# Hybrid decoder layer, prompt and samples together: a fourth buffer for cached keys and values, sample values in four steps, a rearranged tail

## The chip, the cores and the metric

The kernel runs on one core of a Trainium2 chip. A core has five engines with an instruction queue each: TensorE (PE; its weight loads are listed as PEld), VectorE (DVE), ScalarE (ACT), GpSimd (POOL) and SyncE (SP), which issues most of the transfers. The metric is the time of one execution on the device in microseconds, lower is better. Before the change three runs took 1103.71, 1103.06 and 1101.36 us: median 1103.06.

## The reference

One layer works on a prompt of 512 tokens and on 8 samples of 8 tokens each (64 tokens), with width 1024 and shared weights, all in fp32.

```python
def hybrid_layer(x, mem_k, mem_v, ...):
    u = _rms(x) * g_pre_mix
    proj = u @ w_in
    ...
    mix = jnp.concatenate([y_ssd, h_ml], axis=-1) @ w_out
    x = x + _rms(mix) * g_post_mix
    u = _rms(x) * g_pre_x
    qx = (u @ w_xq).reshape(bsz, length, X_HEADS, X_HEAD_DIM)
    sc = jnp.einsum('blhd,bmhd->bhlm', qx, mem_k) * (X_HEAD_DIM ** -0.5)
    pr = jax.nn.softmax(sc, axis=-1)
    o = jnp.einsum('bhlm,bmhd->blhd', pr, mem_v).reshape(bsz, length, X_WIDTH) @ w_xo
    x = x + _rms(o) * g_post_x
    u = _rms(x) * g_pre_ffn
    f = (jax.nn.silu(u @ w_gate) * (u @ w_up)) @ w_down
    x = x + _rms(f) * g_post_ffn
```

The change lies in the cross-attention and in the last line. The memory has 256 positions, 4 heads of 256. The prompt's memory keys and values are computed (`u @ w_mem_k`, `u @ w_mem_v`, both also outputs); each of the 8 samples brings its own keys and values from a cache, 1 MB of keys and 1 MB of values for each sample. `_rms` divides by the root of the mean square plus 1e-6.

## The kernel before, in words

Activations are held transposed, features on the 128 partitions and the 576 tokens as columns: the prompt in columns 0 to 511, the samples in the last 64. Column halves are worked on one after the other. Each large product is made of three matmuls: an fp32 weight is split into a high part `whi`, cast by ScalarE (line 181), and a rest `wlo`, which VectorE and GpSimd subtract (line 188); the activation likewise. TensorE then forms high·high (L202), high·low (L203) and low·high (L205) for each of the 8 blocks of 128 features, so 24 matmuls make one 128-row output block. Raw weights come in 512 KB loads into a ring of two buffers (`raw`, L176); `whi` and `wlo` have rings of three. A scheduler at build time sets the order of instructions on each engine in most of the program. In the stretches under `tc.manual_schedule` it follows a list of due times written in the kernel.

The cross-attention runs over the heads h = 3, 2, 1, 0. For each head come two query blocks `xq(2h+1)` and `xq(2h)` (24 matmuls each for this column half), the memory keys `mem_key` (48 matmuls, tiles `ps_mk`), the values of the previous head `attn_values` (transposes `ps_pt` and products `ps_ov`), the scores `attn_scores` (`ps_at`) and the memory values `mem_value` (L783 and its neighbours, `ps_v`).

The samples' attention is woven into this. `hb` is a half of the samples, four samples each. `pick` takes for each sample two 512 KB loads of its cached keys or values (`cached`, L1314, issued on SP's queue), and does eight matmuls for it with a 32-column weight (L1327, two trace rows for each matmul), one per head and feature half, that write to four row groups of one PSUM bank. It yields four times in all, after each sample, so a step is two loads, eight matmuls and, after every second sample, the masked adding up by VectorE (L1335, L1337). Two PSUM banks, `B0` and `B1`, take turns. The loads cycle through three places of 4 KB per partition in the tile of slot 5, named `kva` in the trace: each `dma_start` must wait until the matmuls that read its place are done.

`attn_samples_k` is the scores of the samples (`ps_sa`), then softmax and two transposes (`ps_pts`). `attn_samples_v` is the product with the values (`ps_os`), then two transposes (`ps_ots`, L1363) and the copies into `oh` and `ol`, the activations of the output projection. In the loop over h, four `next(steps)` take the steps of `attn_samples_k`: half 1 within h = 2 and half 0 within h = 1. `attn_samples_v` is called whole at the end of h = 1 (half 1) and of h = 0 (half 0); where its instructions then stand on TensorE is for the scheduler to decide.

The output projection `xo` follows: j = 0 to 7, each 24 matmuls of 288 columns (`ps_xo`) in the first column part, weights `wxo`. ScalarE takes squares and the scaled result out of PSUM (L268, L1443). `u3l`, an activation of the FFN stage, takes slot 5 after the sample attention is done with it.

At the end, the down projection's last column part (256 prompt tokens) runs by a list of due times. For each block j, `evac0` adds the partial sums (L2080), squares them (L2083) and scales them by the norm's gain (L2084). `root` sums the squares over the features (L2054), and forms v = sum/1024 + eps (L2057, VectorE) and y = sqrt(v) (L2058, ScalarE); `root_end` makes r ≈ 1/sqrt(v) of it by a reciprocal and one Newton step (L2062 to L2065). `f_rows` transposes the result to tokens on partitions (`ps_ft`, L2114), `last` scales by r and adds the residual (L2130), and the output is stored. One quarter of the output goes through ScalarE (`scaled`) and VectorE (`scaled_add`, L2143) instead.

Of the kernel before, what the change touches and what calls it, by code (L numbers as in the profile page):

```python
# [11 lines left out]
F32 = mybir.dt.float32  # L12
F32R = mybir.dt.float32r
BF16 = mybir.dt.bfloat16
AF = mybir.ActivationFunctionType
ALU = mybir.AluOpType
# [3 lines left out]
P = 128  # L20
# [5 lines left out]
EPS = 1e-6  # L26
# [90 lines left out]
def build(nc, tc, ctx, I, O):  # L117
    V, A, G, S, TE = nc.vector, nc.scalar, nc.gpsimd, nc.sync, nc.tensor
# [12 lines left out]
    def SL(slot, name, dt=F32, shape=(P, KT, T)):  # L131

        return big.tile(list(shape), dt, name=name, tag="s%d" % slot, bufs=1)
# [30 lines left out]
    def PAR(k, j=None, w=1):  # L164
        a, b = _cols[k]
        return par[:, a:b] if j is None else par[:, a + j:a + j + w]

    ident, identb, sel, ones = C32("ident"), C16("identb"), C16("sel"), C32("ones")
# [136 lines left out]
    for k in range(KT):  # L305
        if k % 2 == 0:
            c = slice(128 * k, 128 * k + 256)
# [6 lines left out]
        if k % 2 == 0:  # L314
# [4 lines left out]
                                     op0=ALU.mult, op1=ALU.subtract)  # L319
# [244 lines left out]
    y = xs  # L564
# [100 lines left out]
    for g in range(2):  # L665
        ps = BP("ps_xts")
# [5 lines left out]
    ps = BP("ps_bts")  # L672
# [7 lines left out]
    for g in range(2):  # L680
        for hb in range(2):
            dst = cpad[:, g, 4 * hb:4 * hb + 4, :].rearrange("p b t -> p (b t)")
            src = bc[:, 2 + g, TP + 32 * hb:TP + 32 * hb + 32]
# [4 lines left out]
    for g in range(2):  # L688
# [13 lines left out]
        for h in range(8):  # L702
            k, j = h % 2, (8 * g + h) // 2
# [6 lines left out]
    ps = BP("ps_eg")  # L710
# [7 lines left out]
    for b in range(4):  # L718
# [9 lines left out]
        for hb in range(2):  # L728
# [4 lines left out]
            for g in range(2):  # L733
                ps = BP("ps_hu")
# [6 lines left out]
    ps = BP("ps_yt")  # L741
# [89 lines left out]
    for h in range(4):  # L831
# [17 lines left out]
        for c in range(4):  # L849
# [3 lines left out]
                        op=ALU.mult)  # L853
        num = mp_.tile([P, 4, 257], F32, name="num", tag="num", bufs=2)
        for c in range(4):
# [10 lines left out]
            else:  # L866
                V.scalar_tensor_tensor(cn[:, 0:257], cprev[:, 0:257], scalem[:, c, h:h + 1], psc[:, 0:257],
                                       op0=ALU.mult, op1=ALU.add)
# [42 lines left out]
    for hb in range(2):  # L911
        r = slice(32 * hb, 32 * hb + 32)
# [5 lines left out]
        for b in range(4):  # L918
# [9 lines left out]
            for h in range(4):  # L928
                ps = BP("ps_cu")
                mm(ps[:, 0:258], km[:, h * P:(h + 1) * P], vst[:, h * 258:(h + 1) * 258], start=True, stop=True)  # L930
                V.scalar_tensor_tensor(cn[:, h, :], c0[:, h, :], es[:, h, 8 * bb + 7:8 * bb + 8], ps[:, 0:258],
                                       op0=ALU.mult, op1=ALU.add)
# [94 lines left out]
    for j in range(8):  # L1027
        hm = qk[:, 4 * (j % 2) + j // 2, 0:TP]
        with tc.issue_after((evs[0] if j > 2 else htc).ins):
            A.activation(mixm_h[:, j, 0:TP], hm, AF.Copy, scale=ghalf[:, j:j + 1])  # L1030
        V.scalar_tensor_tensor(mixm_l[:, j, 0:TP], hm, ghalf[:, j:j + 1], mixm_h[:, j, 0:TP].bitcast(F32),
                               op0=ALU.mult, op1=ALU.subtract)
# [160 lines left out]
    m = out2(7, 0)  # L1193
    with tc.issue_after(m.ins):
        rc = rstd_cols([ssq], HCHUNKS[1], "po1", alloc=B0)
    m = out2(6, 0)
# [9 lines left out]
    s5 = SL(5, "kva", F32, (P, 4608))  # L1206
# [98 lines left out]
            split(oh[:, j, 0:TP], ol[:, j, 0:TP], pso)  # L1305


    kv = [s5[:, 1024 * i:1024 * i + 1024] for i in range(3)]
    turn = [0]

    def cached(src):
# [5 lines left out]
    def pick(dst, hb, src, lhs, name):  # L1317

        for pair in range(2):
            ps = (B0, B1)[pair](name)  # L1320
            for b2 in range(2):
                b = 2 * pair + b2
                o = ps[:, 256 * b2:256 * b2 + 256]
                for d in range(2):
                    t_ = cached(src[4 * hb + b, :, d])
                    for h in range(4):
                        mm(o[32 * h:32 * h + 32, :], lhs(h, d), t_[:, h, :], start=d == 0, stop=d == 1,  # L1327
                           skip_group_check=True)
                if not b2:
                    yield  # L1330
            for b2 in range(2):
                b = 2 * pair + b2
                o = ps[:, 256 * b2:256 * b2 + 256]
                if b == 0:
                    V.tensor_scalar(dst, o, C32("bmask")[:, 0:1], None, op0=ALU.mult)  # L1335
                else:
                    V.scalar_tensor_tensor(dst, o, C32("bmask")[:, b:b + 1], dst, op0=ALU.mult, op1=ALU.add)  # L1337
            if not pair:
                yield

    def attn_samples_k(hb):
        pr, pt = s5[:, 3072 + 256 * hb:3328 + 256 * hb], s5[:, 3584 + 256 * hb:3840 + 256 * hb]
        yield from pick(pr, hb, I["kc"], lambda h, d: qsm[:, 2 * h + d, 32 * hb:32 * hb + 32], "ps_sa")
        mx = at.tile([P, 1], F32, name="mxs")
        sm = at.tile([P, 1], F32, name="sms")
        V.reduce_max(mx, pr, axis=AX.X)
        V.tensor_scalar(mx, mx, -1.0 / 16.0, None, op0=ALU.mult)
        A.activation(pr, pr, AF.Exp, scale=1.0 / 16.0, bias=mx, accum_out=sm)
        V.reciprocal(sm, sm)
        V.tensor_scalar(pr, pr, sm, None, op0=ALU.mult)  # L1350
        pst = (B0, B1)[hb]("ps_pts")
        for m in range(2):
            TE.transpose(pst[:, m * P:(m + 1) * P], pr[:, m * P:(m + 1) * P], ident)
        A.copy(pt, pst[:, 0:256])

    def attn_samples_v(hb):
        pt, ot = s5[:, 3584 + 256 * hb:3840 + 256 * hb], s5[:, 4096 + 256 * hb:4352 + 256 * hb]
        tt = slice(TP + 32 * hb, TP + 32 * hb + 32)
        for _ in pick(ot, hb, I["vc"], lambda h, m: pt[:, m * P + 32 * h:m * P + 32 * h + 32], "ps_os"):
            pass  # L1360
        pst = (B0, B1)[hb]("ps_ots")
        for dv in range(2):
            TE.transpose(pst[:, dv * P:(dv + 1) * P], ot[:, dv * P:(dv + 1) * P], ident)  # L1363
        p4 = pst[:, 0:256].rearrange("p (d h t) -> p h d t", d=2, h=4)
        oh4 = oh[:, :, tt].rearrange("p (h d) t -> p h d t", d=2)
        ol4 = ol[:, :, tt].rearrange("p (h d) t -> p h d t", d=2)
        A.copy(oh4, p4)
        V.tensor_tensor(ol4, p4, oh4.bitcast(F32), op=ALU.subtract)

    mk, m = mem_key(3, wm[:2])  # L1370
    with tc.issue_after(m.ins):
        rc = rstd_cols([ssq], HCHUNKS[0], "po0", alloc=B0)
    mv, m = mem_value(3, wm[2:])
# [10 lines left out]
    m = xq(4, 1)  # L1384
    with tc.issue_after(m.ins):
        rc2[1] = rstd_cols([ssq2], HCHUNKS[1], "p21", alloc=B1)
    m = xq(5, 1)
    with tc.issue_after(m.ins):
        rstd_rows(rc2[1], HCHUNKS[1], rb2, B1)
    m = xq(6, 1)  # L1390
    with tc.issue_after(m.ins):
        rc2[0] = rstd_cols([ssq2], HCHUNKS[0], "p20", alloc=B1)
    m = xq(7, 1)
# [6 lines left out]
    steps = iter(())  # L1400
    for h in range(3, -1, -1):

        xq(2 * h + 1, 0)
        next(steps, None)
        xq(2 * h, 0)
        next(steps, None)
        if last:
            mk = mem_key(h)
            next(steps, None)
            attn_values(*last)  # L1410
            next(steps, None)
        pr = attn_scores(h, mk)
        if last:
            mv = mem_value(h)
        last = h, pr, mv
        if h > 1:
            steps = attn_samples_k(h - 2)
        else:
            attn_samples_v(h)
    attn_values(*last)  # L1420
    st.close()

# [23 lines left out]

    u3_ = SL(3, "u3h", F32R, (P, 5120))
    u3h = u3_[:, 0:KT * T].rearrange("p (k t) -> p k t", t=T)
    u3l = SL(5, "u3l", F32R)
    rb, rb3 = rb_tile("px_rb"), rb_tile("p3_rb")  # L1450
    ssq3 = ssq_tile("ssq3")
    x_d = dr.tile([P, KT, T], F32, name="x_d")
# [4 lines left out]
    for j in range(8):  # L1457
        step = xo(j, 0, wx if 3 < j < 7 else None)
        if j < 3:

            step(0, KT - 2)
            with tc.issue_after(ends[-1].ins) if j else ExitStack():
                ends.append(step(KT - 2, KT)[0])
        else:
            ends.append(step(0, KT)[0])


    plan = []

    def at_(p, fn, *a):  # L1470
        plan.append((p, len(plan), lambda: fn(*a)))
# [177 lines left out]
    for n_, (key, p) in enumerate(order):  # L1649
        src = I[{"xo": "wxo", "g": "wgate", "u": "wup"}[key[0]]][key[1]]  # L1650
# [315 lines left out]
    with tc.manual_schedule(engines={TE.engine, A.engine, V.engine, G.engine, S.engine}):  # L1966
# [4 lines left out]
        fp = ctx.enter_context(tc.tile_pool(name="ffn", bufs=1, reuse_waits="tile"))  # L1971
        gt = fp.tile([P, 8, 288], F32, name="gt")
        sw = fp.tile([P, 1024], F32, name="sw")
# [8 lines left out]
    f2 = SL(4, "f_ffn")  # L1982
# [62 lines left out]

    plan = []
    tail, squares = {}, {}

    def root(name, terms, chunks):

        n, ps = len(chunks), B0("ps_ss")
        for m, (t_, b) in enumerate(terms):
            for c, (t0, _) in enumerate(chunks):
                mm(ps[:, c:c + 1], t_[:, t0 - b:t0 - b + P], ones, start=m == 0 and c == 0, stop=m == len(terms) - 1, skip_group_check=True)  # L2054
        v, y, a, r = [fp.tile([P, n], F32, name=name + k) for k in ("_v", "_y", "_a", "_r")]
        tail[name] = v, y, a, r
        V.tensor_scalar(v, ps[:, :n], 1.0 / 1024.0, EPS, op0=ALU.mult, op1=ALU.add)  # L2057
        A.activation(y, v, AF.Sqrt)  # L2058

    def root_end(name):  # L2060
        v, y, a, r = tail[name]
        V.reciprocal(y, y)  # L2062
        V.tensor_tensor(a, y, y, op=ALU.mult)
        V.scalar_tensor_tensor(a, a, -0.5, v, op0=ALU.mult, op1=ALU.mult)
        V.scalar_tensor_tensor(r, a, 1.5, y, op0=ALU.add, op1=ALU.mult)  # L2065
        tail[name] = r

    def root_rows1():
# [9 lines left out]
    def evac0(j):  # L2078
        fj = f2[:, j, 0:256]
        V.tensor_tensor(fj, fj, tail[j], op=ALU.add)  # L2080
        if j:
            squares[j] = ph.tile([P, 320], F32, name="sq", tag="sq", bufs=2)[:, :256]
        A.activation(squares[j] if j else ssqf[:, 0:256], fj, AF.Square)  # L2083
        A.activation(fj, fj, AF.Copy, scale=PAR("g_postffn", j))  # L2084

    def sum0(j):
        V.tensor_tensor(ssqf[:, 0:256], ssqf[:, 0:256], squares[j], op=ALU.add)
# [20 lines left out]
    parts = [(c, d) for c in range(2) for d in range(2)]  # L2108
    xr, xt, ft = [], {}, {}

    def token_rows(src, i, ps):
        c, d = parts[i]
        for j in range(4):
            TE.transpose(ps[:, j * P:(j + 1) * P], src[:, 4 * d + j, c * P:(c + 1) * P], ident)  # L2114
        return ps.rearrange("p (j k) -> p j k", j=4)

    def x_rows(i):
# [4 lines left out]
    def x_copy(i):  # L2122
        A.copy(*xt[i])

    def f_rows(i):
        ft[i] = token_rows(f2, i, (MP if i % 2 else GP)("ps_ft"))

    def last(i):
        o, rc = xt[i][0], tail["pf0"][:, parts[i][0]:parts[i][0] + 1]
# [16 lines left out]
    for i in range(4):  # L2146
        at_(4.0 + i, x_rows, i)
        at_(4.55 + i, x_copy, i)
        at_((7.35, 8.7)[i % 2] + i / 100, f_rows, i)
    at_(8.4, lambda: root("pf0", [(ssqf, 0), (squares[7], 0)], HCHUNKS[0]))  # L2150
    at_(8.8, root_end, "pf0")
    at_(9.0, scaled)
# [115 lines left out]
```

## Time and profile before

| | |
|---|---|
| runs, median (lowest to highest) | 1103.06 us (1101.36 to 1103.71) |
| the profiled execution's own time | 1101.67 us |
| its span in the trace | 1099.9 us |
| granted TensorE clock | 0.998 of full |
| TensorE busy | 1088.4 us (99%), 8355 matmuls |
| VectorE busy | 755.0 us (69%) |
| ScalarE busy | 610.4 us (55%) |
| GpSimd busy | 229.9 us (21%) |
| loads of cached keys (values) | 16 (16) of 512 KB, median 6.4 (7.1) us from issue to landing |

How to read it: the profiled execution is one execution with the hardware's profiler on. Its span, from the first instruction to the last, is 1.8 us less than its own time. Matmuls are pipelined: the row of one matmul shows the time from its start until its result is through, which is longer than the distance to the start of the next. So TensorE's real pace is read from start to start, and a "busy" share of 99% still contains short waits. In a row of the timeline the brackets give the idle time before it and what ended it. The chain that ended last is a walk back from the last instruction, at each step to whatever released it; its shares add up to the span.

### The profile page before, as it was taken

To read this page: it belongs to the slowest core of one execution; us is meant where nothing else is said; L and a number is where in the kernel's file an instruction comes from. 1 tells how busy PE (TensorE), PEld (TensorE's weight loads), DVE (VectorE), ACT (ScalarE), POOL (GpSimd) and SP (SyncE) were. 2 spreads that over 40 slices of the span, in tenths; PEclk is the share of its full clock that TensorE was granted. 3 is DMA by queue.
4 is the path that set the end of the run, shared out by engine and by line. 5 is a ranking of instruction groups with operands and counts; after the bars stand their busy time and mean duration, and the time that the engine had idled before them with its cause. 6 is when DMAs were issued, how large, how long until landed. Compare 5 with 4: busy or idle time off the path is not lost.

```text
span 1099.9 us, 21201 instructions
## 1 busy us (share of the span) xinstructions
PE 1088.4 (99%) x8355; PEld 1041.6 (95%) x8355; DVE 755.0 (69%) x1506; ACT 610.4 (55%) x1106; POOL 229.9 (21%) x305
## 2 busy tenths in 40 slices
PE   9999999999999999999999999999999999999997
PEld 9999888998999999999988889999999999999997
DVE  6896776558877764669655456676567877787555
ACT  6877523346654564656444445645467467656654
POOL 1443544223212112000233301100011111111000
PEclk9999999999999999999999999999999999999999
DMA  6775544334745348653468755644475777678532
GB/s 208 189 150 126 154 144 154 125 96 146 208 140 158 82 152 276 206 201 97 160 234 287 264 188 182 223 154 104 115 175 138 157 187 171 140 174 194 122 129 87
DMA packets 58536, 181.29 MB, mean 165 GB/s; under 512 B 6428, under 2 KB 11676, under 8 KB 57924
## 3 DMA queue, kind: packets, MB, share of 16 engines
q1 hardware_dynamic: 42308, 136.88, 37.5%
q0 software_dynamic: 15552, 41.95, 19.6%
q8 instruction: 65, 1.06, 0.4%
q10 hardware_dynamic: 576, 1.11, 0.3%
q14 instruction: 35, 0.29, 0.1%
HBM read 159.26 MB, written 20.65 MB: 164 GB/s over the span
## 4 chain that ended last, share of the span: by engine, by line
PE 95%; DMA 3%; DVE 1%; ACT 0%; issue 0%; DVEq 0%; ACTq 0%
PE ps_in L202 7%; PE ps_in L203 7%; PE ps_in L205 6%; PE ps_o L202 3%; PE ps_o L205 3%; PE ps_o L203 3%; PE ps_u L1777 3%; PE ps_u L1779 3%; PE ps_u L1778 3%; PE ps_g L1777 3%; PE ps_g L1779 3%; PE ps_g L1778 3%; PE ps_v L784 2%; PE ps_v L783 2%; PE ps_v L782 2%; PE ps_dn L1777 2%
## 5 line engine op out<-in xcount | busy, mean ns | idle before, releaser
L202 PE MATMUL ps_in<-uh,whi 128*128 128x320 f32 (+1 forms) x544 | 163.6, 301 | 0.0
L205 PE MATMUL ps_in<-uh,wlo 128*128 128x320 f32 (+1 forms) x544 | 163.5, 301 | 0.0
L203 PE MATMUL ps_in<-ul,whi 128*128 128x320 f32 (+1 forms) x544 | 162.6, 299 | 0.0
L181 ACT CAST whi<-raw 128x1024 fp32r<-128x1024 f32 (+1 forms) x102 | 102.8, 1011 | 91.6 <-PE ps_in L203 28.5
L188 DVE TENSOR_TENSOR wlo<-raw,whi 128x512 fp32r<-128x512 f32 (+1 forms) x94 | 94.6, 1007 | 62.9 <-ACT whi L181 54.5
L202 PEld LDWEIGHTS ps_in<-uh,whi 128*128 128x128 f32 x544 | 103.2, 190 | 2.3 <-issue 1.7
L205 PEld LDWEIGHTS ps_in<-uh,wlo 128*128 128x128 f32 x544 | 103.0, 190 | 1.1 <-issue 0.4
L203 PEld LDWEIGHTS ps_in<-ul,whi 128*128 128x128 f32 x544 | 103.1, 190 | 0.6
L186 POOL DMA_DIRECT2D wlo<-win x32 | 27.8, 877 | 86.8 <-ACT wlo L185 78.7
L1777 PE MATMUL ps_u<-b,whi 128*128 128x288 f32 x144 | 42.5, 296 | 0.0
L1778 PE MATMUL ps_g<-b,whi 128*128 128x288 f32 x144 | 42.4, 295 | 0.0
L1778 PE MATMUL ps_u<-b,whi 128*128 128x288 f32 x144 | 42.4, 295 | 0.0
L1777 PE MATMUL ps_g<-b,whi 128*128 128x288 f32 x144 | 42.2, 296 | 0.0
L202 PE MATMUL ps_xo<-qh,whi 128*128 128x288 f32 x128 | 38.6, 303 | 0.0
L1750 ACT CAST whi<-rawx 128x1024 fp32r<-128x1024 f32 (+1 forms) x26 | 25.6, 986 | 23.4 <-PE ps_dn L1778 13.0
L202 PE MATMUL ps_o<-mixs_h,whi 128*128 128x320 f32 (+1 forms) x128 | 38.2, 298 | 0.0
L205 PE MATMUL ps_o<-mixm_h,wlo 128*128 128x256 f32 (+1 forms) x128 | 38.1, 298 | 0.0
L203 PE MATMUL ps_xq<-u2l,whi 128*128 128x320 f32 (+1 forms) x128 | 38.1, 299 | 0.0
L203 PE MATMUL ps_o<-mixm_l,whi 128*128 128x256 f32 (+1 forms) x128 | 38.0, 297 | 0.0
L202 PE MATMUL ps_o<-mixm_h,whi 128*128 128x256 f32 (+1 forms) x128 | 37.9, 296 | 0.0
L205 PE MATMUL ps_xq<-u2h,wlo 128*128 128x320 f32 (+1 forms) x128 | 37.9, 296 | 0.0
L202 PE MATMUL ps_xq<-u2h,whi 128*128 128x320 f32 (+1 forms) x128 | 37.8, 299 | 0.0
(762 smaller groups left out, 3919.1 us busy)
## 6 DMA issues: line engine op xcount, KB each, us to landing
raw<-win SPq DMA_DIRECT2D x35, 512.0 KB, 3.7
raw<-wout SPq DMA_DIRECT2D x17, 512.0 KB, 3.9
kva<-kc SPq DMA_DIRECT2D x16, 512.0 KB, 6.4
kva<-vc SPq DMA_DIRECT2D x16, 512.0 KB, 7.1
raw<-wxq SPq DMA_DIRECT2D x13, 512.0 KB, 3.5
raw<-wgate SPq DMA_DIRECT2D x13, 512.0 KB, 5.8
raw<-wup SPq DMA_DIRECT2D x13, 512.0 KB, 4.9
wlo<-win POOLq DMA_DIRECT2D x24, 256.0 KB, 5.5
```

What stands on the lines that cost most here:

```text
L181: A.copy(hi[:, :n], raw[:, :n])
L186: G.dma_start(lo[:, a:b], src[:, a:b], accum_op=ALU.add)
L188: e.tensor_tensor(lo[:, a:b], raw[:, a:b], hi[:, a:b].bitcast(F32), op=ALU.subtract)
L202: mm(ps, wh, ah, start=i == 0, stop=False)
L203: mm(ps, wh, al, start=False, stop=False)
L205: m = mm(ps, tiles[order[c]][1], xh(order[c], t0, n), start=False, stop=c == len(tiles) - 1)
L782: mm(o, ah, hi[:, j:j + 256], start=k == 0, stop=False, skip_group_check=True)
L783: mm(o, al, hi[:, j:j + 256], start=False, stop=False, skip_group_check=True)
L1750: A.copy(s.h3[:, s.all], s.r2[:, s.all])
L1777: mm(ps, wh, b[0][k], start=start and k == 0, stop=False, skip_group_check=True)
L1778: mm(ps, wh, b[1][k], start=False, stop=False, skip_group_check=True)
L1779: m = mm(ps, wl, b[0][k], start=False, stop=k == nk - 1, skip_group_check=True)
```

## The change

Three things are changed.

1. The cached keys and values get a fourth place, a tile `kvb` from a pool of its own that is closed after the first column part of the output projection. `u3l` is allocated after that.
2. `attn_samples_v` yields as `attn_samples_k` does. Half 1's steps are taken within h = 0 and half 0's within the output projection, one after each `xo(j, 0)`, j = 0 to 7 (as long as there are any).
3. In the tail, `root` lets ScalarE take the square root from PSUM directly (scale 1/1024, eps as a bias tile), and VectorE forms v and its reciprocal; `root_end` has three operations instead of four. For block j = 7 the scaled copy is VectorE's, into another buffer, instead of ScalarE's in place. Of the transposes for odd i, the first three blocks are due before the root's sums (8.2), the last one after them (8.7).

```diff
-    kv = [s5[:, 1024 * i:1024 * i + 1024] for i in range(3)]
+    kxs = ExitStack()
+    kx = kxs.enter_context(tc.tile_pool(name="kx", bufs=1, side="right", reuse_waits="tile"))
+    kv = [s5[:, 1024 * i:1024 * i + 1024] for i in range(3)] + [kx.tile([P, 1024], F32, name="kvb")]
...
     def attn_samples_v(hb):
...
-        for _ in pick(ot, hb, I["vc"], lambda h, m: pt[:, m * P + 32 * h:m * P + 32 * h + 32], "ps_os"):
-            pass
+        yield from pick(ot, hb, I["vc"], lambda h, m: pt[:, m * P + 32 * h:m * P + 32 * h + 32], "ps_os")
...
         last = h, pr, mv
-        if h > 1:
-            steps = attn_samples_k(h - 2)
-        else:
-            attn_samples_v(h)
+        steps = attn_samples_k(h - 2) if h > 1 else attn_samples_v(h)
     attn_values(*last)
...
-    u3l = SL(5, "u3l", F32R)
...
             ends.append(step(0, KT)[0])
+
+        next(steps, None)
+    kxs.close()
+    u3l = SL(5, "u3l", F32R)
...
+    eps = fp.tile([P, 1], F32, name="eps")
+    V.memset(eps, EPS)
...
         tail[name] = v, y, a, r
+        A.activation(y, ps[:, :n], AF.Sqrt, scale=1.0 / 1024.0, bias=eps)
         V.tensor_scalar(v, ps[:, :n], 1.0 / 1024.0, EPS, op0=ALU.mult, op1=ALU.add)
-        A.activation(y, v, AF.Sqrt)
+        V.reciprocal(v, v)
 
     def root_end(name):
+
         v, y, a, r = tail[name]
-        V.reciprocal(y, y)
-        V.tensor_tensor(a, y, y, op=ALU.mult)
-        V.scalar_tensor_tensor(a, a, -0.5, v, op0=ALU.mult, op1=ALU.mult)
-        V.scalar_tensor_tensor(r, a, 1.5, y, op0=ALU.add, op1=ALU.mult)
+        V.tensor_tensor(a, y, v, op=ALU.mult)
+        V.scalar_tensor_tensor(r, a, -0.5, y, op0=ALU.mult, op1=ALU.mult)
+        V.scalar_tensor_tensor(r, r, 1.5, a, op0=ALU.add, op1=ALU.mult)
         tail[name] = r
...
         A.activation(squares[j] if j else ssqf[:, 0:256], fj, AF.Square)
-        A.activation(fj, fj, AF.Copy, scale=PAR("g_postffn", j))
+        if j < 7:
+            A.activation(fj, fj, AF.Copy, scale=PAR("g_postffn", j))
+        else:
+            V.tensor_scalar(sw[:, 512:768], fj, PAR("g_postffn", j), None, op0=ALU.mult)
...
-    def token_rows(src, i, ps):
+    def token_rows(src, i, ps, js=range(4)):
         c, d = parts[i]
-        for j in range(4):
-            TE.transpose(ps[:, j * P:(j + 1) * P], src[:, 4 * d + j, c * P:(c + 1) * P], ident)
+        for j in js:
+            t_ = sw[:, 512 + c * P:640 + c * P] if src is f2 and 4 * d + j == 7 else src[:, 4 * d + j, c * P:(c + 1) * P]
+            TE.transpose(ps[:, j * P:(j + 1) * P], t_, ident)
...
-        at_((7.35, 8.7)[i % 2] + i / 100, f_rows, i)
+        if i % 2:
+
+            at_(8.2 + i / 100, f_rows, i, range(3))
+            at_(8.7 + i / 100, f_rows, i, range(3, 4))
+        else:
+            at_(7.35 + i / 100, f_rows, i)
```

More of the change, by code (lines that the diff above doesn't have):

```diff
@@ L2123, in x_copy, with f_rows @@
         A.copy(*xt[i])
-    def f_rows(i):
-        ft[i] = token_rows(f2, i, (MP if i % 2 else GP)("ps_ft"))
+    def f_rows(i, js=range(4)):
+        if 0 in js:
+            tail["ft", i] = (MP if i % 2 else GP)("ps_ft")
+        ft[i] = token_rows(f2, i, tail["ft", i], js)
     def last(i):
```

## The prediction

> **What bounds the kernel now.** I read the page first, its chain of work, then the chain of waits and TensorE's timeline around the lines that change.
>
> ```profile
> span 1099.9 us, 21201 instructions
> ...
> PE 95%; DMA 3%; DVE 1%; ACT 0%; issue 0%; DVEq 0%; ACTq 0%
> ```
>
> TensorE sets the end; transfers own 3% of the chain. No matmul is removed, so only time in which TensorE stands still, and the tail behind its last matmul, can be won. The chain between 540 and 670 us shows where it stands still in the changed region (start, length, what):
>
> ```profile
> 579.55 6.03 DMA kva<-kc
> ...
> 594.36 5.98 DMA kva<-kc
> ...
> 612.10 6.05 DMA kva<-vc
> ...
> 637.50 5.84 DMA kva<-vc
> ...
> 655.52 1.23 DVE wlo L188
> 656.76 3.58 DMA raw<-wxo
> 660.36 1.06 ACT whi L181
> 661.50 1.24 DVE wlo L188
> ```
>
> Each piece of 6 us runs from the issue of a load to its landing; TensorE worked through most of it. What it lost is read from the matmul before each place and the one that waited (start, length, engine, line, operation):
>
> ```profile
> 584.90 0.28 PE L205 MATMUL ps_mk<-memhl,wlo 128*128 128x256 f32 x1
> 585.63 0.64 PE L1327 MATMUL ps_sa<-kva,qsm 128*32 128x256 f32 x8 [0.45 <-DMA kva<-kc]
> ...
> 600.00 0.28 PE L1276 MATMUL ps_at<-mk,qh 128*128 128x256 f32 x1
> 600.38 0.64 PE L1327 MATMUL ps_sa<-kva,qsm 128*32 128x256 f32 x8
> ...
> 616.76 0.28 PE L202 MATMUL ps_mk<-memhl,whi 128*128 128x256 f32 x1
> 618.19 0.64 PE L1327 MATMUL ps_os<-kva 128*32 128x256 f32 x8 [1.14 <-DMA kva<-vc]
> ...
> 643.02 0.29 PE L205 MATMUL ps_xo<-qh,wlo 128*128 128x288 f32 x1
> 643.38 0.64 PE L1327 MATMUL ps_os<-kva 128*32 128x256 f32 x8
> ...
> 662.12 0.29 PE L203 MATMUL ps_xo<-ql,whi 128*128 128x288 f32 x1
> 662.77 0.40 PE L205 MATMUL ps_xo<-qh,wlo 128*128 128x288 f32 x1 [0.36 <-DVE wlo L188]
> ```
>
> The normal distances, and what a burst of sample matmuls costs, come from undisturbed places:
>
> ```profile
> 578.52 0.28 PE L203 MATMUL ps_xq<-u2l,whi 128*128 128x256 f32 x1
> 578.64 0.28 PE L205 MATMUL ps_xq<-u2h,wlo 128*128 128x256 f32 x1
> 578.86 1.07 PE L1327 MATMUL ps_sa<-kva,qsm 128*32 128x256 f32 x16
> 579.86 0.39 PE L202 MATMUL ps_xq<-u2h,whi 128*128 128x256 f32 x1
> ...
> 546.31 1.05 PE L1327 MATMUL ps_sa<-kva,qsm 128*32 128x256 f32 x10
> 547.29 0.39 PE L1274 MATMUL ps_at<-mk,qh 128*128 128x256 f32 x1
> ```
>
> A 256-column matmul starts 0.12 us after the one before; the entry into a burst takes 0.22. Start to start less about 0.21 (0.23 and 0.13 among 288-column matmuls), the five places lose 0.52, 0.17, 1.22, 0.13 and 0.52: 2.56 us, 2.04 of it on cached keys and values, the last on a weight of the output projection. That is all there is to win here: 0.23% of the time.
>
> **The change part by part.** *Fourth place and values in steps.* All sixteen loads of keys and sixteen of values stay, with their 128 matmuls. A step takes two loads; with four places a step's pair is issued as the step two before it lets go of its places, so it has one whole step and the work between. For the fourth step of a head that work is 48 matmuls of the memory keys (5.8 us), a 16-row step (1.0) and the transposes of the text's weights (about 1 us), with entries about 8.1 us from the end of step two, and the first place is let go half a step earlier. What stands against it is SP's one queue:
>
> ```profile
> 580.54 4.48 SPq L176 DMA_DIRECT2D raw<-wmv  x2
> 585.11 0.38 SPq L1314 DMA_DIRECT2D kva<-kc  x1
> ...
> 582.87 1.79 POOL L188 TENSOR_TENSOR wlo<-raw,whi 128x512 fp32r<-128x512 f32 x1 [4.06 <-ACT whi L181]
> ...
> DMA to landing us min/median/max: 3.8/6.7/8.0
> ```
>
> For h=1 the second wmv load stands in the queue ahead of the pair of step four and must wait until POOL has read the raw buffer (582.87 + 1.79 = 584.66). So the pair goes out at 585.1 and 585.5 as the single load did before. Step two begins near 583.0 (24 matmuls after 579.9), step four at about 592.0, its second load is wanted at 592.5. By the median of 6.7 us the loads land at 591.8 and 592.2 and nothing waits; by the maximum of 8.0, at 593.5, the wait is 1.0. Bounds 0 and 1.0; the last of several stacked loads is nearer the maximum than the first, so I take **0.4**, in place of 0.52 + 0.17. Queued behind a waiting matmul is all of TensorE. h=2 has no second weight ahead of its pair (none). For h=0:
>
> ```profile
> 614.53 0.72 SPq L1314 DMA_DIRECT2D kva<-vc  x1
> ```
>
> the pair is issued there around 614.1 and 614.5, and with 6.7 us lands at 620.8 and 621.2; step four needs it from 621.8 on. The 1.22 goes. At the maximum of 8.0 it would keep 0.3 to 0.7. The values of h=0 are spread over the projection and loaded from about 639.5, wanted from 649.6: the 0.13 goes. The projection's weight chain (655.52 to 662.74 in the chain above) starts when the block j=0 is done; a burst that stood ahead of that end now stands behind it, about 1.3 us of cover against 0.52 of wait: that goes too. If not, 0.52 stays. So 2.56 is removed and 0.4 returns.
>
> *Bursts.* Two rows are one matmul here. Sixteen rows take 1.00 us (578.86 to 579.86; the row's 1.07 has 0.07 of pipeline behind it), so eight take 0.64 − 0.07 = 0.57 (row 585.63) and eight more add 0.43. What a burst costs beside its rows is then 0.57 − 0.43 = 0.14 within, 0.10 at the entry (0.22 for 0.12) and about 0.1 at the exit (the matmul behind it 0.39 long for 0.28): about 0.33. The changed program has 22 bursts for 24: −0.66. But in the projection they are cut to 6, 2, 2, 4, 3 and 7 matmuls, and the ten rows at 546.31 took 0.98, as much as sixteen: a group of four matmuls that is not full costs as a full one (0.43). The six odd bursts hold 24 matmuls, six groups, and take up eight: +0.86. I take the sum of the two, **+0.2**, with −0.66 and +0.86 as ends. The first load of the fourth place is issued some 150 us early, beside the loads of the output weights; no matmul there waits for a load that it delays by more than its slack. Price 0; uncovered, one load's 0.38 us issue.
>
> *The tail.* VectorE's, ScalarE's and TensorE's rows of before:
>
> ```profile
> 1092.25 0.16 DVE L2057 TENSOR_SCALAR pf_v<-ps_ss 128x2 f32<-128x2 f32 x1 [1.15 <-PE ps_ss L2054]
> 1092.68 0.17 DVE L2062 RECIPROCAL pf_y<-pf_y 128x2 f32<-128x2 f32 x1 [0.27 <-ACT pf_y L2058]
> ...
> 1093.28 0.16 DVE L2065 SCALAR_TENSOR_TENSOR pf_r<-pf_a,pf_y 128x2 f32<-128x2 f32 x1
> 1093.47 0.75 DVE L2130 SCALAR_TENSOR_TENSOR raw<-ps_ft,pf_r,raw 128x512 f32<-128x512 f32 x1
> ...
> 1091.14 0.42 ACT L2083 ACTIVATE sq<-f_ffn 128x256 f32<-128x256 f32 x1 [2.00 <-DVE f_ffn L2080]
> 1091.59 0.51 ACT L2084 ACTIVATE f_ffn<-f_ffn,par 128x256 f32<-128x256 f32 x1
> 1092.44 0.20 ACT L2058 ACTIVATE pf_y<-pf_v 128x2 f32<-128x2 f32 x1 [0.35 <-DVE pf_v L2057]
> ...
> 1092.08 1.07 PE L2114 MATMUL ps_ft<-c,f_ffn 128*128 128x128 f32 x8
> ```
>
> From the root's sum to the last scaling lie 1.22 us: v (0.19 with its gap), root (0.24), reciprocal and three products (0.20 each). The edit means the root on ScalarE and v with its reciprocal on VectorE to run side by side; then the chain is the longer arm (0.39) and three products, 0.99: −0.24. But in the changed program's order VectorE's v waits for ScalarE's root, because both read the same bank of PSUM. Root, v, reciprocal and three products stand in a row again: 1.23, and up to 0.09 more if the bias given as a tile costs what the scale given as a tile costs (0.51 against 0.42). I take **+0.05**, ends −0.24 and +0.10. The Trainium skill, "PSUM — Partial Sum Buffer", section "PSUM bank collisions raise a hardware error", says why that wait has to be there: ScalarE and VectorE may not touch one bank at a time and nothing arbitrates. By that rule the sum is +0.05, without it −0.24; no run here shows the collision.
>
> The moved copy for j=7 fits VectorE's idle 1.15 us before v (0.42 wanted). The earlier transposes fill TensorE's pause before the sums; they were done at 1093.15 anyway, before the factor at 1093.45, so that gains nothing. Without the cover the copy would cost its 0.42.
>
> **Sum.** −2.56 + 0.4 + 0.2 + 0.05 = −1.9 us. The profiled execution took 1101.67 (span 1099.9, 1.8 around it), which becomes 1099.8. It lies 1.4 under the median of the runs, 1103.06, and on that the sum gives **1101.1**.
>
> **The rivals.** *All gains come:* no wait is left, bursts gain 0.66 and the tail's two readers run in parallel: −2.56 − 0.66 − 0.24 = −3.5, 1099.6. For it: 0.4 and 0.2 are small corrections that I chose between ends. Against: the order of the tail.
>
> *The waits only move:* loads now go in pairs, so the second of a pair lands later than a single load would. With 8.0 us for the last one, 1.0 is lost in h=1 and in h=0 each, 0.52 stays at the weight: −2.56 + 2.5 + 0.25 = +0.2, 1103.3. That is the case in which the change does not do what it says. For it: the maximum in the row; against: 6.0 us in the chain.
>
> *Slower:* one mechanism, SP's queue. The two wmv loads, the pair of step three and that of step four are six transfers in a row.
>
> ```profile
> 637.00:644.00 7.00, 6.93 (x70) 5.57 (x62) 2.83 (x5) 3.23 (x8) 1.04 (x1) 1.00 0.82 249
> ```
>
> The last column is GB/s: at 249 a load of 0.524 MB takes 2.11 us. The first out at 580.0 lands after 3.58 (the wxo row); five more at 2.11 end at 594.1, against 592.5 wanted: 1.6 lost, in h=2, h=1 and h=0 each. With the 0.52 that stays: −2.56 + 4.8 + 0.5 + 0.25 = +3.0, 1106.1. It loses 2.2 us or more from 2.06 us for a load on. Against it: single loads stacked up landed after 6 us, not 8.
>
> **How the numbers follow.** A measurement of this kernel tells no change from one of 0.2%, 2.2 us. Forecast 0.50, its own range 1100.2 to 1102.1 by the ends of its terms (faster 0.22, within 0.28). All gains 0.25 (0.24 and 0.01). Waits move 0.11 (within 0.10, slower 0.01). Queue 0.14 (within 0.02, slower 0.12). Together faster 0.46, within 0.41, slower 0.13. The range takes in all gains with the terms' ends below it and half of the way to the queue's case: 1098.6 to 1104.6.
>
> **What would show it.** Right: no wait for a vc load near 618, at most 0.5 us for a kc load near 592, none before the weight wlo at the projection's j=5; in the tail the root starts first, v after it, and 1.2 to 1.3 us lie between the sums' end and the scaling. Wrong: loads of a pair landing 8 us after issue or more, TensorE waiting at step three of a head, new waits for wmk or wmv weights behind the pairs, root and v at the same time, or 22 bursts that take other than about 18 us.

## The result and the profile after

The changed kernel takes 1100.28 us (median of 18 runs, 1099.13 to 1102.85) beside 1103.09 us for the kernel before (18 runs, 1100.28 to 1105.20). The ratio is 0.9977 with a 95% interval of 0.9969 to 0.9984: 1.8 to 3.4 us faster. The forecast was 1101.1, with a gain of 1.9.

The profiled execution of the changed kernel took 1102.09 us, one of its longest, where that of before, with 1101.67, was one of its shorter ones. So the two first traces, laid side by side, show a loss. The page after:

```profile
span 1100.3 us, 21200 instructions
...
PE 94%; DMA 3%; DVE 1%; POOL 1%; ACT 0%; SPq 0%; issue 0%; DVEq 0%; ACTq 0%; POOLq 0%
```

The span is 0.4 us longer than before's, and transfers still own 3% of the chain. TensorE's timeline shows where (start, length, engine, line, operation, idle time before it and its releaser):

```profile
592.02 0.64 PE L1329 MATMUL ps_sa<-kva,qsm 128*32 128x256 f32 x8 [0.56 <-DMA kva<-kc]
592.59 0.39 PE L782 MATMUL ps_v<-whi,memhl 128*128 128x256 f32 x1
594.07 0.64 PE L1329 MATMUL ps_sa<-kvb,qsm 128*32 128x256 f32 x8 [1.10 <-DMA kvb<-kc]
...
624.29 0.38 PE L782 MATMUL ps_v<-whi,memhl 128*128 128x256 f32 x1
625.38 0.42 PE L1329 MATMUL ps_os<-kvb,kva 128*32 128x256 f32 x4 [0.71 <-DMA kvb<-vc]
```

The waits at 585, 600, 618 and 643 of before are gone. New ones stand at the fourth step of h=1 (0.62 and 1.27 us beyond the normal distance, start to start) and of h=0 (0.88): 2.77 us, against 2.04 in the first trace of before. The chain of waits of the same execution says where these loads come from:

```profile
581.85 1.79 POOL wlo L188
...
583.66 0.33 SPq L176
...
584.08 0.39 SPq L1316
...
584.56 9.46 DMA kvb<-kc
...
614.17 1.79 POOL wlo L188
...
615.99 0.33 SPq L176
...
616.41 0.53 SPq L1316
...
616.98 8.35 DMA kvb<-vc
```

Both times GpSimd frees the raw buffer, SP then issues the second wmv load and behind it the pair of the fourth step, and the last of the stack lands 8 to 9.5 us after its issue.

A second thing happens after 594 in this trace. The view by windows (stretch, length, then busy time of PE, PEld, DVE, ACT and POOL, granted clock, DMA share, GB/s):

```profile
592.00:594.00 2.00, 0.95 (x9) 0.34 (x9) 1.04 (x3) 1.32 (x3) 2.00 (x2) 1.00 0.48 188
594.00:595.20 1.20, 1.13 (x12) 0.72 (x13) 1.20 (x3) 0.06 (x1) 0.82 (x2) 0.93 0.94 140
595.20:598.40 3.20, 3.20 (x15) 3.01 (x15) 1.74 (x5) 1.26 (x2) 1.79 (x1) 0.50 0.91 289
598.40:600.00 1.60, 1.60 (x9) 1.34 (x8) 0.52 (x2) 0.39 (x2) 0.00 (x0) 0.99 1.00 384
```

For 3.2 us and a little more behind the two waits TensorE was granted half its clock, and its matmuls of 256 columns started 0.21 us apart instead of 0.12. From the matmul behind the second wait (594.64) to the first one behind the next head's first burst (611.69) it took 17.05 us; the same stretch of the second trace below takes 15.50. So the half clock cost another 1.5 us.

In the tail the root stands ahead of v, and everything else stands behind both:

```profile
1092.59 0.27 ACT pf_y L2060
...
1092.89 0.17 DVE pf_v L2061
...
1093.08 0.18 DVE pf_v L2062
...
1093.28 0.17 DVE pf_a L2067
...
1093.67 0.17 DVE pf_r L2069
...
1093.87 1.41 DVE raw L2140 x2
```

From the root to the scaling it is 1.28 us; it was 1.22 from v to the scaling.

### The profile page after: what moved, and what is told of

Read it like the earlier page. It is cut to its first block, busy times and chain, and to the rows that moved or that the text cites. A ratio compares the mean times of both kernels' runs of the same rounds, so it can differ in the third digit from the quotient of the medians.

```text
span 1100.3 us, 21200 instructions
## 1 busy us (share of the span) xinstructions
PE 1087.7 (99%) x8355; PEld 1042.2 (95%) x8355; DVE 754.1 (69%) x1508; ACT 611.2 (56%) x1105; POOL 230.3 (21%) x305
## 3 DMA queue, kind: packets, MB, share of 16 engines
q10 hardware_dynamic: 576, 1.11, 0.3%
## 4 chain that ended last, share of the span: by engine, by line
PE 94%; DMA 3%; DVE 1%; POOL 1%; ACT 0%; SPq 0%; issue 0%; DVEq 0%; ACTq 0%; POOLq 0%
PE ps_in L202 7%; PE ps_in L203 7%; PE ps_in L205 6%; PE ps_o L202 3%; PE ps_o L205 3%; PE ps_o L203 3%; PE ps_u L1778 3%; PE ps_u L1780 3%; PE ps_u L1779 3%; PE ps_g L1778 3%; PE ps_g L1779 3%; PE ps_g L1780 3%; PE ps_v L783 2%; PE ps_v L784 2%; PE ps_v L782 2%; PE ps_dn L202 2%
```

## The experiments

The kernels come in three groups, and those of a group ran on the same chip and share their runs of before: the first four, then the next four, then the last three. A time is compared with before only within its group.

### Attention alone, tail alone

The one is the changed kernel with the old lines from `plan = []` of the tail to the end of `build`, the other is before with the new ones.

> The changed kernel with the old tail: fourth place and stepped values only. Theory A (the gain is made in the attention, where waits for cached keys and values shrink; the tail costs 0.05 to 0.1 us): about 1100.2, 2.9 us under before. Rival B (the profiled execution of the changed kernel is typical: the waits only moved to the fourth step of h=1 and h=0, the attention loses 1 us, and the gain comes from the tail): about 1104, 1 us over before.

Measured: 1100.30 us against 1103.08; ratio 0.9975 (0.9962 to 0.9987).

> The kernel before with the new tail only. Theory A: 1103.1 to 1103.2, no difference that can be told; in the profile the root comes first, v waits for it, and the stretch from the end of the sums to the scaling is 1.28 us where it was 1.22. Rival B: about 1099 to 1100, with the stretch near 1.0 us or another piece of the tail shorter by microseconds.

Measured: 1103.14 us against 1103.08; ratio 1.0000 (0.9991 to 1.0009); 1.28 us from the start of the root to the scaling. Theory A holds in both: the gain is the attention's, and the tail's share is within 1 us of nothing. Rival B, to which the first trace of the changed kernel pointed, falls.

### Fourth place alone, steps alone

```diff
 fourth_only: changed kernel, old tail, and
-        yield from pick(ot, hb, I["vc"], ...)
+        for _ in pick(ot, hb, I["vc"], ...):
+            pass
...
-        steps = attn_samples_k(h - 2) if h > 1 else attn_samples_v(h)
+        if h > 1:
+            steps = attn_samples_k(h - 2)
+        else:
+            attn_samples_v(h)
 vsteps_only: changed kernel, old tail, and
-    kv = [...] + [kx.tile([P, 1024], F32, name="kvb")]
+    kv = [...]
```

> The kernel before with the fourth place only: values still called whole, old tail. Theory A with the place as its main cause: the waits near 585 and 600 for keys shrink, the one near 618 for values shrinks by half: 1 to 2 us under before, 1101 to 1102. If the steps of the values are the main cause: within 0.7 us of before.

Measured: 1100.40 us against 1103.08; ratio 0.9974 (0.9963 to 0.9984). More than expected: the place alone gives as much as the whole change. Of the waits its trace keeps 0.39 us at the fourth step of h=1 and 0.63 near 614, where before had 1.22.

> The kernel before with the values in steps only: three places, old tail. If the steps are the main cause: the wait of 1.2 us near 618 goes and so does the one of the projection's weight, 1 to 2 us under before. If the place is needed for them: the second load of each step can be issued only when the step before is done, so each stepped pair waits as the keys did (0.5 and 0.2 us), and the time stays within 0.7 us of before.

Measured: 1103.66 us against 1103.08; ratio 0.9998 (0.9988 to 1.0009). The steps give nothing without the place that can be told, and, since the attention with both takes 1100.30 and the place alone 1100.40, nothing with it either.

Its trace shows half the clock again, behind a single wait. TensorE's timeline, then the windows, of the steps alone:

```profile
584.49 0.28 PE L205 MATMUL ps_mk<-memhl,wlo 128*128 128x256 f32 x1
586.43 0.42 PE L1327 MATMUL ps_sa<-kva,qsm 128*32 128x256 f32 x4 [1.66 <-DMA kva<-kc]
```

```profile
586.40:587.60 1.20, 1.17 (x13) 0.76 (x14) 0.46 (x1) 0.00 (x0) 0.00 (x0) 1.00 0.91 335
587.60:590.80 3.20, 3.20 (x18) 3.20 (x17) 1.20 (x4) 1.55 (x2) 0.65 (x1) 0.52 0.99 388
```

### Second traces of both kernels

> The kernel before once more, for a second trace. Theory A (the waits for cached loads differ from execution to execution with the speed of the transfers, and the first trace of before was one with short waits): the wait near 585 is 1 us or more where it was 0.5, those near 618 and 643 together over 2 us where they were 1.35, and the time lies above that of the first trace, near 1103. Rival (the waits are fixed by the program and the spread of the times comes from elsewhere): the same waits within 0.1 us.

Measured: 1102.41 us. TensorE's timeline of this execution of before, at the four places of the first one:

```profile
584.70 0.28 PE L205 MATMUL ps_mk<-memhl,wlo 128*128 128x256 f32 x1
586.22 0.42 PE L1327 MATMUL ps_sa<-kva,qsm 128*32 128x256 f32 x4 [1.24 <-DMA kva<-kc]
...
600.59 0.28 PE L1276 MATMUL ps_at<-mk,qh 128*128 128x256 f32 x1
601.19 0.41 PE L1327 MATMUL ps_sa<-kva,qsm 128*32 128x256 f32 x2 [0.32 <-DMA kva<-kc]
...
617.56 0.28 PE L202 MATMUL ps_mk<-memhl,whi 128*128 128x256 f32 x1
618.66 0.64 PE L1327 MATMUL ps_os<-kva 128*32 128x256 f32 x8 [0.81 <-DMA kva<-vc]
...
643.50 0.29 PE L205 MATMUL ps_xo<-qh,wlo 128*128 128x288 f32 x1
645.08 0.42 PE L1327 MATMUL ps_os<-kva 128*32 128x256 f32 x4 [1.29 <-DMA kva<-vc]
```

Start to start less 0.21 (0.23 among 288 columns) these are 1.31, 0.39, 0.89 and 1.35: 3.94 us where the first trace had 2.04. The places are fixed by the program, the sizes are not. Theory A holds; 618 and 643 together are 2.24. The trace of the tail alone, with the same attention, has 1.72, 1.73 and 1.10, 4.55 us.

> The changed kernel once more, for a second trace. Theory A: its waits at the fourth step of h=1 and of h=0, 2.8 us together in the first trace, are shorter, 1 to 2 us, and the time is near 1100.3. Rival: 2.8 us again.

Measured: 1099.16 us. The same two places of the changed kernel as above:

```profile
592.03 0.38 PE L782 MATMUL ps_v<-whi,memhl 128*128 128x256 f32 x1
592.43 0.64 PE L1329 MATMUL ps_sa<-kvb,qsm 128*32 128x256 f32 x8
...
621.09 0.38 PE L782 MATMUL ps_v<-whi,memhl 128*128 128x256 f32 x1
622.27 0.64 PE L1329 MATMUL ps_os<-kvb,kva 128*32 128x256 f32 x8 [0.79 <-DMA kvb<-vc]
```

0.17 and 0.97: 1.14 us, and no stretch at half the clock.

### The fourth step later, and wmk's split by VectorE alone

```diff
 late_fourth: changed kernel, and attn_values returns its last product
-            attn_values(*last)
+            behind[0] = attn_values(*last)
             next(steps, None)
+            behind[0] = None
...
 in pick
+                    with tc.issue_after(behind[0].ins) if behind[0] else ExitStack():
                     for h in range(4):
                         mm(...)
 wmk_dve: changed kernel, and in mem_key
-            split_w(I["wmk"][2 * h + kk])
+            split_w(I["wmk"][2 * h + kk], cut=1024)
```

> The changed kernel with the fourth step's matmuls put behind the products of attn_values, some 4 us of TensorE's work later; loads are issued as before. If the remaining waits are of loads that land too late for the fourth step (theory A): they go, 1 to 2 us under the changed kernel, about 1098.5 to 1099.3. If places that come free later make the next head's loads late: 1100 to 1101, with new waits at the first step of the next head.

Measured: 1098.88 us against 1104.04; ratio 0.9951 (0.9933 to 0.9970). TensorE's timeline at h=1's fourth step:

```profile
597.82 0.39 PE L1304 MATMUL ps_ov<-prh,mv 128*128 128x512 f32 x1
598.13 0.64 PE L1332 MATMUL ps_sa<-kva,qsm 128*32 128x256 f32 x8
598.59 0.61 PE L1332 MATMUL ps_sa<-kvb,qsm 128*32 128x256 f32 x8
```

The burst follows the products at once; no wait for a cached load over 0.1 us is left in the attention, and the next head's first step has none either. The loads did not come earlier: the pair for h=1 was issued at 585.57 and 586.05, where the changed kernel's first trace has 584.08 and 584.56. They were late for a step that need not have stood so early.

> The changed kernel with the rest of the memory keys' weights subtracted by VectorE alone (wmk: cut 1024 instead of half on GpSimd), so that the raw buffer comes free about 0.5 us earlier and the loads behind it on SP's queue are issued earlier. If SP's queue behind the second wmv load sets the landing of the fourth pair: 0.3 to 0.8 us under the changed kernel. If the transfers themselves do (all queues full): the same as the changed kernel within 0.3 us, or slower where VectorE is needed for something else.

Measured: 1098.82 us against 1104.04; ratio 0.9946 (0.9928 to 0.9965). The chain of waits of this kernel, then of the attention alone:

```profile
583.64 9.26 DMA kvb<-kc
```

```profile
584.67 8.30 DMA kvb<-kc
```

Issued 1.03 us earlier than in the attention alone, the load landed at 592.90 against 592.97, and the waits at the fourth steps stayed (1.23, 1.12 and 0.47 us). That the transfers themselves set the landing, and not the moment of issue, fits this pair of executions but isn't shown by it: with the issue within 0.1 us the first trace of the changed kernel has this load land 1 us later (584.56 + 9.46 = 594.02). The time is 1.5 us under the changed kernel's 1100.28, which ran in another comparison, more than either theory had; the trace doesn't show where. What this edit gives is open.

> The changed kernel beside the two variants of it on the same chip, and a third trace of it. Theory A: near 1100.3, 2.5 to 3 us under before; waits at the fourth steps of 1 to 3 us in all.

Measured: 1101.59 us against 1103.50; ratio 0.9983 (0.9972 to 0.9993), with waits of 0.09 and 1.02 at the fourth steps. The time missed the expected 1100.3 and the gain the expected 2.5 to 3; the interval overlaps that of the first comparison.

> The changed kernel with both edits: fourth step behind attn_values, and the memory keys' weights split by VectorE alone. If both act on the same wait for the fourth pair: 1098.5 to 1099, the same as each alone. If wmk's split gains something of its own besides: 1097.5 to 1098.3.

Measured: 1099.51 us (five runs) against 1103.50; ratio 0.9963 (0.9951 to 0.9975), 2.1 us under the changed kernel (twelve runs) in the same group. This is above both expectations. Against before it isn't better than either edit alone, which ran in another group, so both may well act on one wait; that isn't shown. Of the variants only this one was timed beside the changed kernel. The single edits are compared with it through before: ratios of 0.9951 and 0.9946 beside 0.9977 and 0.9983.

### Two banks for the last root

```diff
-        n, ps = len(chunks), B0("ps_ss")
+        n, ps, ps2 = len(chunks), B0("ps_ss"), (B1("ps_s2") if name == "pf0" else None)
...
-        A.activation(y, ps[:, :n], AF.Sqrt, scale=1.0 / 1024.0, bias=eps)
+        A.activation(y, (ps if ps2 is None else ps2)[:, :n], AF.Sqrt, scale=1.0 / 1024.0, bias=eps)
```

The sums of each term are formed in both banks, `ps` first.

> The changed kernel with the last root's sums formed twice, in two PSUM banks, one for ScalarE's root and one for VectorE's v (two more matmuls of one column per term). If the shared bank is what puts root and v in a row: both start within 0.3 us of one another, and from the end of the first bank's sums to the scaling it is 1.0 to 1.15 us instead of 1.28. If something else orders them: 1.28 or more. The time of the whole tells nothing at this size.

Measured: 1099.96 us in one run. VectorE's and ScalarE's timelines:

```profile
1090.42 0.16 DVE L2062 TENSOR_SCALAR pf_v<-ps_ss 128x2 f32<-128x2 f32 x1 [1.08 <-PE ps_ss L2058]
1090.61 0.17 DVE L2063 RECIPROCAL pf_v<-pf_v 128x2 f32<-128x2 f32 x1
1091.16 0.16 DVE L2068 TENSOR_TENSOR pf_a<-pf_y,pf_v 128x2 f32<-128x2 f32 x1 [0.38 <-ACT pf_y L2061]
...
1091.74 0.75 DVE L2141 SCALAR_TENSOR_TENSOR raw<-ps_ft,pf_r,raw 128x512 f32<-128x512 f32 x1
...
1090.86 0.26 ACT L2061 ACTIVATE pf_y<-ps_s,eps 128x2 f32<-128x2 f32 x1 [1.47 <-PE ps_s L2058]
```

v starts as its own sums end, 0.44 us ahead of the root: the shared bank was what put them in a row. From the root to the scaling it is 0.88 us instead of 1.28. But the second pair of sums takes TensorE 0.46 us, more than I had allowed for, so from the end of the first bank's sums it is 1.36: missed, and nothing is won. The attention of this kernel is that of the changed one; its waits at the fourth steps are 0.10 and 0.67 us.

## Why the prediction was right, and where it was not

**Direction and place: right.** The gain is made where TensorE waits for cached loads, and the tail gives nothing that can be told (1.0000). The forecast's 1.9 lies in the measured 1.8 to 3.4, near its lower end; the medians differ by 2.8.

**"That is all there is to win here" (2.56 us): mis-sized.** The places were right, the sizes were those of one execution. Waits for cached loads in three traces with three places (before, its second trace, the tail alone) are 2.04, 3.94 and 4.55 us, 3.5 on the mean. In five with the changed attention (first and second trace, attention alone, timed beside the variants, two banks) they are 2.77, 1.14, 2.30, 1.11 and 0.77, 1.6 on the mean. So about 1.9 us of them go, where the sum had 1.6 (2.04 − 0.4). That these two are close is luck: both what stood there and what is left were much larger than the sum had them.

**"The 1.22 goes" (h=0): wrong.** I had the pair issued at 614.1 and 614.5, landing after the median of 6.7 us, before step four needs it (from 621.8). Issue and need came about as I had them. The second wmv load does stand ahead of this pair as well, which I didn't see, but in the four traces that no half clock had delayed the second load of the pair still goes out at 613.92 to 614.19, and step four could use it from 621.3 to 621.9 on. (The 616.98 of the first trace stands behind 3 us of waits and half clock.) What failed is the landing. The chain of the second trace, then of the attention alone:

```profile
613.92 8.30 DMA kvb<-vc
```

```profile
614.19 9.09 DMA kvb<-vc
```

In all five traces the last load of this stack took 8.3 to 9.1 us, more than the longest of before (8.0), and 0.88, 0.97, 1.42, 1.02 and 0.67 us are left. For h=1 the prediction did say that the last of several stacked loads is nearer the maximum than the first; for h=0 it went by the median, and the stack is the same.

**0.4 us at h=1: too small.** The same five traces show 1.89, 0.17, 0.88, 0.09 and 0.10, 0.6 on the mean. The upper bound of 1.0 came from the longest landing of before, 8.0 us; 9.46 came up.

**0.13 at 643 and 0.52 at the projection's weight: right.** Both are gone in the changed kernel. With the place alone 0.44 of the weight's wait stays in its trace, and three waits of about 0.4 us that before doesn't have stand near the start of the projection. So the steps do something there, but it is too little to be told in the times.

**Bursts, +0.2: wrong in the balance.** From the first sample burst to the first FFN matmul, less the waits for cached loads and for the projection's weight, it is 150.8 to 151.0 us in the three traces of the old attention (153.54 − 2.56, 155.27 − 4.38, 155.70 − 4.92) and 150.3 to 150.5 in four of the changed one (151.41 − 1.14, 152.62 − 2.30, 151.40 − 1.11, 151.23 − 0.77): about 0.5 less, not 0.2 more. The time inside the bursts rose as forecast, from 17.52 to 18.06; distances behind and between them fell by more. Which of them, I did not follow. Put together, 1.9 of cached loads, 0.4 of the weight and 0.5 here come to the 2.8 of the medians, as far as means of three and five traces can tell, and with the half clock of the first trace left out.

**Tail, +0.05: right**, 0.06 by the profile, for the reason given: root and v in a row. The rule of the Trainium skill that the prediction set beside it, "PSUM — Partial Sum Buffer", section "PSUM bank collisions raise a hardware error", agrees with the two-bank run in this: with a bank each, v no longer waits for the root. That a collision would fault, no run here shows. The moved copy and the earlier transposes gained nothing, as forecast.

**The rivals.** "All gains come" (1099.6) is as near to the measured 1100.28 as the forecast (1101.1), so the time doesn't decide against it. The traces do: 1.6 us of waits are left, the bursts' own time rose, and the tail's two readers stand in a row. "The waits only move" is true of h=0's last pair and of single executions, but not of the mean. "Slower" named the right stack on SP's queue: its last load does land after 8 to 9.5 us. It was priced too high: no trace shows a loss in all three heads at once. Two of the signs that the prediction gave for being wrong did appear, a load of a pair landing after 8 us or more, and a wait at a kc load near 592 of over 0.5 us (1.27 in the first trace). Both come from the landing that was mis-sized; the gain came out all the same, because the kernel before waits longer than the sum had it.

## What to carry to other kernels

Waits for transfers differ from execution to execution; one profile gives their places, and a sum made of their sizes needs the traces of several. When a buffer lets more loads stand in a row, redo the issue order of each queue for every pass of the loop, and give the last load of a stack the time that stacked loads take: here 8.3 to 9.5 us, where the median of all was 6.7. And where a late load cannot be issued earlier, ask whether its consumer may run later; that took the rest of the waits here, and its trace shows no new one.

## What the hardware showed unexpectedly

A wait on TensorE can cost more than its length. Behind waits of 0.62 and 1.27 us close together, and in another kernel behind one of 1.73 us, the granted clock was 0.50 and 0.52 for 3.2 us. It did not follow every time: the tail alone has two waits of 1.7 us with the clock at 1.00 behind them. The Trainium skill, "TensorE: Matmul & The Clock Gate", section "What's actually happening", tells of a clock that is halved by how busy TensorE was in a free-running window of about 3.4 us. The length agrees: the traces' clock records have half clock for 3.41 us in both kernels, from 595.03 and from 587.71 on, and in all thirteen traces the first stretch at full clock lasts a whole number of 3.413 us (583.68, 590.51, 1085.44, 1088.85 or 1092.27), so the window does run on a grid of its own. But there it takes an idle window, while here the 3.4 us ahead of each change were only about half idle (TensorE busy for 1.88 us from 591.6 to 595.0, and for 1.74 from 584.3 to 587.7). Why the tail alone was spared stays open: on its grid the same stretch, 584.3 to 587.7, has the same 1.74 us.

The times may show this too. Of the 21 runs of before in the second group, the two with a mean granted clock of 0.994 took 1107.5 and 1113.6 us, and the eight with 0.998 took 1101.4 to 1104.5. A clock lower by 0.004 is 4.4 us of the whole, about what the first of the two has too much; it leaves half of the second's 9.5 us over the median unexplained, and there is no trace of either run.
